# Weights and token chunks laid out as they lie on chip, and another order of the opening loads, splits and sums of squares

## The chip, the cores and the metric

One core of a Trainium2 chip runs the whole program. The metric is device time in microseconds (us) of that core; the kernel before takes 1963.29 us, the median of 3 runs (1960.71 to 1966.26). Engines are named as the profile names them: PE is TensorE, PEld its weight loads, DVE VectorE, ACT ScalarE, POOL GpSimd, SP the engine that issues every DMA of this kernel. A suffix q (SPq) marks an issue queue.

## The reference

One layer of a streaming encoder. `x_prompt` (2048 tokens of 1024), `x_sample` (32 tokens) and 16 meta tokens are normalised (RMSNorm with gain `norm_g`) and go through one input projection `w_in` of 1024 x 4104:

```
u = rmsnorm(h, g_norm) @ w_in     # columns q_A k_A v_A g_A | q_B k_B v_B g_B | 8 forget values
oa = stick-breaking attention of 8 heads (A); ob = forgetting (softmax with decay) attention of 8 heads (B)
h = h + concat(oa * silu(ga), ob * silu(gb)) @ w_out
```

The prompt attends to itself behind the meta tokens, the sample also to 2048 cached rows. The outputs are the normalised `h`, all new k and v rows, and the log forget values. Everything is float32.

## The kernel before

All 2096 tokens lie in one reversed list: prompt, sample, meta. Every projection is done with split operands: a float32 value is written as a high part (rounded to the format that TensorE multiplies at full rate) and a low part (the rest), and `mm3` (line 259) does three matmuls, high x high, high x low and low x high, for each of the 8 slices of 128 of the 1024 inputs. A group is therefore 24 matmuls into one PSUM bank.

The weights come in units of 256 columns (`load_unit`, line 178): two for each of q, k, v, g of both groups, and four of `w_out`. The first v unit of group B, v10, has 8 columns more, the forget values, which lie elsewhere in `w_in` and come in a second DMA. A unit is loaded in two halves (four slices of 128 rows each, so 1 KB pieces for each partition and slice), and each slice is split by ACT (line 205, the high part times the gain) and DVE (line 206, the low part). The half's raw buffer, `wraw`, exists once; for v10 the second half goes into `raw1`, one of two `raw` buffers that it shares with the token chunks.

The first section, v1, is the v projection of group B. The generator `feed` (line 1491) brings the tokens in 17 chunks of 128 (the last has 48). For chunk t it loads `x_T` into a `raw` buffer (4 KB for each partition), writes the high part (ACT, line 1504) and the low part (DVE, line 1505), squares both halves (ACT, line 1508), adds them up (three adds on POOL, lines 1509 to 1512), and some chunks later `root` sums over partitions with two small matmuls (`ptx`, line 1519) and finds the reciprocal root by a Newton step on DVE and ACT. The result of a group is copied out of PSUM with that root as scale (line 400), so a bank is free only when the chunk's root is there. PSUM has four banks for these groups.

The split chunks stay on chip ("resident") for v1, k1 and q1. `Pace` hands out the steps of `feed` against the steps of the projection: `advance(NL)` before the loop emits the first chunks, then every slice of matmuls advances it a little. Before all that, 40 matmuls on constant data (line 1549) run while the first loads come in. Later sections (k0, v0, q0, g0) fill the forgetting attention (`fx`), g1 and the output projections fill the stick-breaking attention; they read the tokens again through `stream` (line 606), in chunks of about 260 tokens from `x_K`, which is laid out as (128, 8, 2096), so a chunk comes in 1 KB pieces.

The order in which the code emits instructions is a priority. A scheduler then fixes the order on each engine from durations that it assumes, and may move an instruction ahead of earlier ones that wait; on chip each engine works strictly in that fixed order. Only in q1 are DVE and PE held to the order of the code.

Of the kernel before, what the change touches and what calls it, by code (L numbers as in the profile page):

```python
# [7 lines left out]
F32 = mybir.dt.float32  # L8
# [3 lines left out]
ALU = mybir.AluOpType  # L12
# [10 lines left out]
KT = 8  # L23
# [55 lines left out]
@with_exitstack  # L79
def trunk_step_kernel(ctx, tc, x_all, x_T, x_K, ca_kT, ca_v, cb_kT, cb_v, cb_lfT, norm_g, w_in, b_f, w_out,  # L80
                      final_g, ident_c, mask_c, smask_c, rows_c, pick_c,
# [7 lines left out]
    def dma(out, in_):  # L89
        nc.sync.dma_start(out=f32(out), in_=f32(in_))  # L90
# [86 lines left out]

    def load_unit(src, cols, kt, nm, g=None, raw1=None):

# [5 lines left out]
        def load(i):  # L185
            if i and raw1 is not None:
                raw[i] = raw1
# [93 lines left out]
    class SecT(Units):  # L281
        def __init__(self, nm, base, chunks, src, acc, evac, ahead=None, lead=0):
            super().__init__()
            self.nm, self.base, self.chunks, self.src, self.acc, self.evac = nm, base, chunks, src, acc, evac
            self.ahead, self.lead = ahead, lead
            self.every = 1 if lead else 2
            self.upto = 0
            self.next = None

        def unit(self, u):  # L290
            b = self.base + 256 * u
            return load_unit([w_in[:, b:b + 256]], 256, KT, f"{self.nm}{u}", g_col)

# [84 lines left out]
    class SecV(Units):  # L378
# [5 lines left out]
        def unit(self, u):  # L384
            s = self.s
            base = SECS * s + 2 * SEC
            cols = [w_in[:, base + 256 * u:base + 256 * u + 256]]
            if s and u == 0:
                cols.append(w_in[:, 2 * SECS:2 * SECS + 8])
            return load_unit(cols, 264 if s and u == 0 else 256, KT, f"v{s}{u}", g_col, self.raw1 if u == 0 else None)  # L390

# [214 lines left out]
    def stream(nm, a, n):  # L606
# [838 lines left out]

    k0 = SecT("k0", SEC, CH_K, stream, ps_a, evac_k(0))
    q0 = SecT("q0", 0, CH_Q, stream, ps_a, evac_q(0))
    v0 = SecV(0, CH_V, stream, ps_a)
    g0 = SecT("g0", 3 * SEC, CH_Q, stream, ps_a, evac_g(0))
    g1 = SecT("g1", SECS + 3 * SEC, CH_Q, stream, ps_a, evac_g(1), ahead_g)  # L1450

    class OutUnits(Units):
# [20 lines left out]
    with ExitStack() as es:  # L1473
# [17 lines left out]
        def feed():  # L1491

            todo = []
            for t in range(NT):
# [12 lines left out]
                for i in range(2):  # L1507
                    nc.scalar.activation(sq[i].rearrange("p (k c) -> p k c", k=4), raw[:, 4 * i:4 * i + 4], AF.Square)
                nc.gpsimd.tensor_tensor(sq[0], sq[0], sq[1], ALU.add)
                nc.gpsimd.tensor_tensor(sq[0][:, :2 * r], sq[0][:, :2 * r], sq[0][:, 2 * r:], ALU.add)  # L1510
                out = n_p.tile([128, 128], F32, tag="ss", name=f"ss{t}", bufs=3)[:, :r]
                nc.gpsimd.tensor_tensor(out, sq[0][:, :r], sq[0][:, r:2 * r], ALU.add)
# [4 lines left out]
                def root(t=t, r=r, ss=out):
                    pt = ps_t.tile([128, SEC], F32, tag="pt", name=f"ptx{t}")
                    nc.tensor.matmul(pt[:r, 0:1], ss, ones_t[:, 0:1], start=True, stop=True)
                    v = n_p.tile([128, 2], F32, tag="rs", name=f"rs{t}")  # L1520
                    newton(v[:r, 0:1], r_all[:r, t:t + 1], v[:r, 1:2], pt[:r, 0:1])
                    rooted.append(t)
                todo.append(root)
                yield 1.0 - HB
            for f in todo:
# [37 lines left out]
        ng.advance(NL)  # L1563
        for c in v1.run():
# [193 lines left out]
```

## Time and profile before

| | |
|---|---|
| median of 3 runs | 1963.29 us (1960.71 to 1966.26) |
| the profiled execution | 1965.0 us, of which the span of the trace is 1963.2 us |
| PE busy | 1885.2 us (96%) |
| DVE, POOL, ACT busy | 1294.2, 1166.6, 1082.2 us |
| granted TensorE clock, mean | 0.985 |
| DMA | 330.51 MB in 260107 packets, mean 168 GB/s |

Busy means that an instruction was running; for PE a busy share near 100% still allows for the lower clock. The granted clock is 1.00 at 2.4 GHz and 0.50 at 1.2 GHz. The idle time in square brackets of a timeline row is how long the engine had waited before that instruction, with what ended the wait.

### The profile page before, as it was taken

Reading aid. Unit: us, or ns where it says so; the run is one execution under the profiler, and the core shown is the slowest. Engines: PE = TensorE matmul, PEld = TensorE weight load, DVE = VectorE, ACT = ScalarE, POOL = GpSimd, SP = SyncE. Lnnn points to the kernel's source line nnn. Section 1 sums busy time; section 2 is a strip of 40 time slices with the busy share of each in tenths; the row PEclk is TensorE's granted clock in tenths of the full one; section 3 lists DMA queues with packets and bytes.
Section 4 is the critical chain, followed back from the end, with each engine's and each line's share of the span. In section 5 each row is a group of like instructions: output and inputs, shape, how many; then the busy total and the mean of one; then the engine's idle time right before and its main releaser. Section 6 shows DMA issues by size and latency. Waiting matters only on the chain.

```text
span 1963.2 us, 35618 instructions
## 1 busy us (share of the span) xinstructions
PE 1885.2 (96%) x11962; PEld 1479.7 (75%) x11962; DVE 1294.2 (66%) x2387; ACT 1082.2 (55%) x2327; POOL 1166.6 (59%) x1755
## 2 busy tenths in 40 slices
PE   8999999999999999999999999999999899999998
PEld 6999998677767777677777788777777666676566
DVE  5436336656674444766665376888878977878976
ACT  5541213454554554544453566776776777777852
POOL 4500003677777877676875676667777667667700
PEclk7999999999999999999999999999999999999999
DMA  6656657566664455566666544565656534434364
GB/s 164 183 134 151 172 155 192 139 186 164 187 165 132 134 171 169 173 200 198 216 201 195 173 152 156 173 213 181 200 167 204 174 123 151 152 109 154 98 206 165
DMA packets 260107, 330.51 MB, mean 168 GB/s; under 512 B 46525, under 2 KB 195094, under 8 KB 253782
## 3 DMA queue, kind: packets, MB, share of 16 engines
q1 hardware_dynamic: 259926, 328.25, 56.6%
q8 instruction: 94, 1.54, 0.3%
q14 instruction: 87, 0.71, 0.1%
HBM read 211.48 MB, written 116.68 MB: 167 GB/s over the span
## 4 chain that ended last, share of the span: by engine, by line
PE 58%; DVE 9%; DMA 5%; ACT 4%; POOL 3%; issue 3%; SPq 1%; DVEq 0%; ACTq 0%; POOLq 0%
PE pob L702 6%; PE poa L702 5%; PE pta L841 4%; PE sb L1151 3%; PE sb L1152 3%; PE smb L1128 3%; DVE wa L748 2%; PE sa L783 2%; PE sa L782 2%; PE psTg L262 2%; PE psTg L263 2%; PE psTg L264 2%; DMA gfa<-gf_s 2%; PE psTq L262 1%; PE psv L262 1%
## 5 line engine op out<-in xcount | busy, mean ns | idle before, releaser
L754 POOL TENSOR_TENSOR wa<-wa,mba 128x512 f32<-128x512 f32 (+1 forms) x320 | 369.4, 1156 | 172.5 <-DVE wa L748 145.3
L1165 POOL TENSOR_TENSOR accb<-accb,pfb 128x512 f32<-128x512 f32 (+1 forms) x256 | 297.4, 1162 | 103.2 <-ACT pfb L1155 75.4
L748 DVE TENSOR_TENSOR_SCAN wa<-sa,wa,ones_r 128x512 f32<-128x512 f32 x192 | 244.3, 1279 | 42.2 <-ACT sa L745 35.0
L1155 ACT ACTIVATE pfb<-sb 128x512 f32<-128x512 f32 (+1 forms) x320 | 176.0, 552 | 156.6 <-PE sb L1152 152.2
L1131 DVE TENSOR_REDUCE mxb<-smb 128x1 f32<-128x512 f32 (+1 forms) x320 | 194.7, 612 | 75.0 <-PE smb L1128 70.4
L844 ACT COPY ptha<-pta 128x512 f32<-128x512 f32 (+1 forms) x320 | 166.5, 526 | 81.1 <-PE pta L841 78.6
L744 ACT ACTIVATE mba<-sa 128x512 f32<-128x512 f32 (+1 forms) x320 | 174.0, 544 | 25.2 <-POOL wa L754 19.9
L841 PE MATMUL pta<-ident,wa 128*128 128x128 f32 x1088 | 173.4, 275 | 5.8 <-ACT ptha L844 3.2
L745 ACT ACTIVATE sa<-sa 128x512 f32<-128x512 f32 (+1 forms) x320 | 173.7, 543 | 0.0
L702 PE MATMUL poa<-ptha,vca 128*64 128x512 f32 (+2 forms) x640 | 157.7, 558 | 10.1 <-ACT ptha L844 9.8
L841 PEld LDWEIGHTS pta<-ident,wa 128*128 128x128 f32 x1088 | 129.7, 140 | 41.1 <-issue 8.2
L782 PE MATMUL sa<-kca,qaa 128*128 128x512 f32 (+3 forms) x352 | 150.3, 427 | 8.8 <-DVE wa L748 7.8
L262 PE MATMUL psTg<-xhg,whig 128*128 128x260 f32 x512 | 148.6, 290 | 0.0
L702 PE MATMUL pob<-pfb,vcb 128*64 128x512 f32 (+1 forms) x640 | 148.6, 569 | 0.0
L264 PE MATMUL psTg<-xhg,wlog 128*128 128x260 f32 x512 | 145.0, 283 | 0.0
L263 PE MATMUL psTg<-xlg,whig 128*128 128x260 f32 x512 | 144.8, 283 | 0.0
L1128 PE MATMUL smb<-k2b,q2b 66*128 66x512 f32 (+1 forms) x320 | 123.2, 385 | 14.3 <-DVE mxb L1131 9.3
L748 DVE TENSOR_TENSOR_SCAN wa<-sa,ones_r,m 128x512 f32<-128x512 f32 (+3 forms) x128 | 111.9, 878 | 36.5 <-ACT sa L745 23.8
L1151 PE MATMUL sb<-qab,kcb 128*128 128x512 f32 (+1 forms) x320 | 123.3, 385 | 0.7 <-ACT pfb L1155 0.7
L783 PE MATMUL sa<-kca,qz 128*128 128x512 f32 (+3 forms) x352 | 121.8, 358 | 0.0
L1152 PE MATMUL sb<-q2b,k2b 70*128 70x512 f32 (+1 forms) x320 | 121.4, 380 | 0.0
L702 PEld LDWEIGHTS poa<-ptha,vca 128*64 128x64 f32 x640 | 41.9, 137 | 86.1 <-issue 38.3
(296 smaller groups left out, 5408.9 us busy)
## 6 DMA issues: line engine op xcount, KB each, us to landing
xlg<-x_s SPq DMA_DIRECT2D x16, 1040.0 KB
xhg<-x_s SPq DMA_DIRECT2D x16, 1040.0 KB
xwk<-in_x_K_dram SPq DMA_DIRECT2D x8, 1048.0 KB
k_s<-kx SPq DMA_DIRECT2D x64, 131.0 KB
xwq<-in_x_K_dram SPq DMA_DIRECT2D x8, 1040.0 KB
x_s<-xhq SPq DMA_DIRECT2D x8, 1040.0 KB
x_s<-xlq SPq DMA_DIRECT2D x8, 1040.0 KB
q_s<-q SPq DMA_DIRECT2D x64, 130.0 KB
```

The lines of the kernel that those rows point to most:

```text
L262: nc.tensor.matmul(out, a_h[k], b_h[k], start=(k == 0), stop=False)
L263: nc.tensor.matmul(out, a_h[k], b_l[k], start=False, stop=False)
L264: nc.tensor.matmul(out, a_l[k], b_h[k], start=False, stop=(k == n - 1))
L702: nc.tensor.matmul(po[64 * side:64 * side + 64, :n], v, p[:, :n], start=first, stop=False)
L748: nc.vector.tensor_tensor_scan(out=w[:, 1:n + 1], data0=ps[:, :n], data1=m01[:, :n] if diag else ones_t[:, 0:1].broadcast_to([128, n]), in ...
L754: nc.gpsimd.tensor_tensor(w[:, :n], w[:, :n], take[:, :n], ALU.mult)
L782: nc.tensor.matmul(out, self.qa[:, bs], k, start=True, stop=False)
L841: nc.tensor.transpose(pt[:, b * 128:b * 128 + 128], self.w[b][:, c:c + 128], ident)
L1128: nc.tensor.matmul(ps[:, :SEC - s0 + m], q2[0:66, bs], k2[0:66, s0:SEC + m], start=True, stop=True)
L1131: nc.vector.tensor_reduce(mx[:, b, kc:kc + 1], ps[:, v0:v0 + nv + m], AX.X, ALU.max)
L1151: nc.tensor.matmul(ps[:, :n], hd.k[kc][:, js], self.qa[:, :n], start=True, stop=False)
L1165: nc.gpsimd.tensor_tensor(self.acc[:, :n], self.acc[:, :n], pf[:, :n], ALU.add)
```

## The change

The host writes two inputs in another order, with no arithmetic. `w_K` holds all 20 units one behind the other, for each partition first the four slices of half 0, then those of half 1; the 8 forget columns stand inside v10. `x_K`, `x_V` and `x_Q` hold the token chunks of `stream` in the same way, one copy for each of the three ways to cut them. A half of a unit is then one DMA of 128 pieces of 4 KB, a chunk one of 128 pieces of about 8 KB. The amount of data is the same.

```diff
-            r3 = raw[i][:, :kt // 2 * cols].rearrange("p (k c) -> p k c", k=kt // 2)
-            c = 0
-            for a in src:
-                w = a.shape[1]
-                dma(r3[:, :, c:c + w], a.rearrange("(i k p) c -> i p k c", p=128, i=2)[i])
-                c += w
+            n = kt // 2 * cols
+            dma(raw[i][:, :n], w_K[:, W_AT[nm] + i * n:W_AT[nm] + i * n + n])
...
-            dma(t["xw"][:, :KT * n].rearrange("p (k t) -> p k t", k=KT), x_K[:, :, a:a + n])
+            x = {"k": x_K, "v": x_V, "q": x_Q}[nm[0]]
+            dma(t["xw"][:, :KT * n], x[:, KT * a:KT * a + KT * n])
```

In `feed`, half of the chunks go into the `hl` staging buffers instead of `raw` (chunks 1, 2, 4, 5, 8, 9, ...), so four chunks can be under way. The squares of a chunk are emitted one chunk later, behind the splits of the next one.

```diff
-                raw = n_p.tile([128, 4 * 264], F32, tag="raw", name=f"xraw{t}")[:, :KT * r]
+                if t == 0 or t == 3 or t > 3 and (t - 4) // 2 % 2:
+                    raw = rawtile(f"xraw{t}")[:, :KT * r]
+                else:
+                    raw = f32(stage2(f"xraw{t}", SEC).rearrange("p x n -> p (x n)"))[:, :KT * r]
...
                 sub(xl, raw, xh)
-                sq = [stage(f"sq{t}_{i}", F32, "sg")[:, :4 * r] for i in range(2)]
...
+                if t == 0:
+                    yield 0.0
+                if last_:
+                    squares(*last_)
+                last_ = (t, r, raw)
                 yield HB
```

At the start there are 16 constant matmuls. Chunk 0 is split ahead of the weights. Both halves of v11, the second unit, are requested after chunk 1 (`NA`) instead of within the loop; both units use `raw` buffers for their second half. `NL`, the chunks emitted ahead of the loop, goes from 3.5 to 4.

```diff
-WARM = 40
+WARM = 16
-NL = 3.5
+NL = 4.0
+NA = 2.0
...
-        v1.raw1 = n_p.tile([128, 4 * 264], F32, tag="raw", name="raw1")
+        v1.raw1 = rawtile
         v1.prepare(0)
         dma(g_col, norm_g)
         v1.prep.pop(0)()
-        dma(ident, ident_c)
         v1.prep.pop(1)()
         next(ng)
-        nc.vector.tensor_copy(ident16, ident)
+        dma(ident, ident_c)
         v1.ready()
         v1.prepare(1)
         ng = Pace(ng)
-        ng.advance(NL)
+        ng.advance(NA)
+        nc.vector.tensor_copy(ident16, ident)
+        v1.prep.pop(0)()
+        v1.prep.pop(1)()
+        ng.advance(NL - NA)
```

## Rows read from the trace of the kernel before

**Rows 1.** The page, part 1: busy us (share of span) xinstructions.
```profile
PE 1885.2 (96%) x11962; PEld 1479.7 (75%) x11962; DVE 1294.2 (66%) x2387; ACT 1082.2 (55%) x2327; POOL 1166.6 (59%) x1755
```
**Rows 2.** Stretches of 10 us: length, engines' busy us (count), clock, DMA share, GB/s.
```profile
20.00:30.00 10.00, 7.31 (x33) 7.00 (x33) 8.01 (x14) 7.04 (x14) 6.85 (x6) 0.50 0.72 180
...
40.00:50.00 10.00, 9.51 (x56) 9.30 (x55) 5.28 (x16) 3.50 (x8) 2.15 (x4) 0.66 0.74 204
```
**Rows 3.** Tiles psv and ptx: count, ns min/median/max, first and last start us.
```profile
L262 PE MATMUL psv<-whiv,xh x272: 276/282/589, 12.7 to 131.7; 128*128 128x264 f32 x64, 128*128 128x256 f32 x64, 128*48 128x264 f32 x4, 128*48 128x256 f32 x4
...
L1519 PE MATMUL ptx<-ones_r,ss x34: 164/250/373, 12.6 to 106.4; 128*128 128x1 f32 x32, 128*48 128x1 f32 x2
```
**Rows 4.** Timeline, PE: first and last matmul of a group at full clock, twice.
```profile
115.10 0.28 PE L262 MATMUL psv<-whiv,xh 128*48 128x264 f32 x1
...
117.88 0.28 PE L264 MATMUL psv<-whiv,xl 128*48 128x264 f32 x1
118.00 0.28 PE L262 MATMUL psv<-whiv,xh 128*128 128x256 f32 x1
...
120.70 0.28 PE L264 MATMUL psv<-whiv,xl 128*128 128x256 f32 x1
```
**Rows 5.** Timeline of the opening: start, duration, engine, line, operation, count, idle before.
```profile
0.80 0.39 SPq L90 DMA_DIRECT2D xraw<-in_x_T_dram  x1
...
1.56 11.18 PE L1549 MATMUL warm<-masks 128*128 128x512 bf16 x40 [1.56 <-DVE masks L143]
...
3.99 2.61 SPq L90 DMA_DIRECT2D raw<-in_w_in_dram  x2
...
4.28 1.04 ACT L1504 CAST xh<-xraw 128x1024 fp32r<-128x1024 f32 x1 [1.98 <-DMA xraw<-in_x_T_dram]
...
5.36 1.22 DVE L93 TENSOR_TENSOR xl<-xraw,xh 128x1024 fp32r<-128x1024 f32 x1 [3.86 <-ACT xh L1504]
...
6.53 5.71 PEld L1549 LDWEIGHTS <-masks 128*128 128x128 bf16 x27 [0.16 <-issue]
...
11.62 1.74 ACT L205 ACTIVATE whiv<-wrawv,g_col 128x264 fp32r<-128x264 f32 x4 [5.24 <-DMA wrawv<-in_w_in_dram]
...
14.33 0.68 SPq L90 DMA_DIRECT2D rows<-in_rows_c_dram  x1
...
17.41 1.73 ACT L205 ACTIVATE whiv<-raw,g_col 128x264 fp32r<-128x264 f32 x4 [4.06 <-DMA raw<-in_w_in_dram]
...
19.70 2.04 SPq L90 DMA_DIRECT2D xraw<-in_x_T_dram  x2
```
**Rows 6.** Stretches of 1 us, columns as in rows 2.
```profile
3.00:4.00 1.00, 1.00 (x4) 0.30 (x2) 0.00 (x0) 0.00 (x0) 0.00 (x0) 1.00 0.98 326
...
9.00:10.00 1.00, 1.00 (x7) 0.41 (x6) 0.00 (x0) 0.00 (x0) 0.05 (x1) 1.00 0.82 103
...
27.00:28.00 1.00, 1.00 (x6) 1.00 (x6) 1.00 (x1) 0.62 (x1) 0.92 (x2) 0.50 0.92 87
```
**Rows 7.** Waits of PE, 0 to 170 us: total us, times, longest us.
```profile
PE psv L262 <- ACT whiv L205: 5.1, 2, 3.5
PE ptx L1519 <- POOL ss L1512: 2.9, 2, 2.7
```
**Rows 8.** Timeline, ACT ahead of the second unit's last split.
```profile
29.59 0.63 ACT L1508 ACTIVATE sq<-xraw 128x512 f32<-128x512 f32 x1 [1.57 <-POOL ss L1512]
...
38.95 0.49 ACT L205 ACTIVATE whiv<-wrawv,g_col 128x256 fp32r<-128x256 f32 x1
```
**Rows 9.** Timeline where q1 ends and k0 begins.
```profile
316.12 1.71 ACT L205 ACTIVATE whik<-wrawk,g_col 128x256 fp32r<-128x256 f32 x4 [5.25 <-DMA wrawk<-in_w_in_dram]
...
320.06 0.50 PE L1128 MATMUL smb<-k2b,q2b 66*128 66x512 f32 x1 [2.97 <-DVE mxb L1131]
```
**Rows 10.** Stretches of 5 us after it, columns as in rows 2.
```profile
320.00:325.00 5.00, 4.94 (x25) 4.89 (x26) 3.62 (x11) 0.42 (x1) 0.63 (x2) 0.66 0.94 237
...
350.00:355.00 5.00, 2.24 (x12) 1.84 (x13) 4.87 (x11) 0.00 (x0) 1.43 (x2) 0.96 0.19 40
```

More of the change, by code (lines that the diff above doesn't have):

```diff
@@ L62 @@
 MW = 2
-NL = 3.5
+NL = 4.0
+NA = 2.0
 LAG = 2
 NR = 5000.0
-WARM = 40
+WARM = 16
 CH_R = [(0, 384), (384, 384), (768, 384), (1152, 384), (1536, 560)]
 CH_V = [(c * 256, 256) for c in range(7)] + [(1792, 304)]
+COLS = {"q0": 0, "k0": SEC, "v0": 2 * SEC, "g0": 3 * SEC, "q1": SECS, "k1": SECS + SEC, "v1": SECS + 2 * SEC,
+        "g1": SECS + 3 * SEC}
+W_AT, W_ALL = {}, 0
+for _nm in [f"{x}{u}" for x in COLS for u in range(2)] + ["o00", "o01", "o10", "o11"]:
+    W_AT[_nm] = W_ALL
+    W_ALL += KT * (264 if _nm == "v10" else 256)
 def f32(ap):
@@ L186, in load @@
             if i and raw1 is not None:
-                raw[i] = raw1
+                raw[i] = raw1()
             else:
@@ L281, in trunk_step_kernel, with __init__ @@
     class SecT(Units):
-        def __init__(self, nm, base, chunks, src, acc, evac, ahead=None, lead=0):
+        def __init__(self, nm, chunks, src, acc, evac, ahead=None, lead=0):
             super().__init__()
-            self.nm, self.base, self.chunks, self.src, self.acc, self.evac = nm, base, chunks, src, acc, evac
+            self.nm, self.chunks, self.src, self.acc, self.evac = nm, chunks, src, acc, evac
             self.ahead, self.lead = ahead, lead
@@ L290, in unit @@
         def unit(self, u):
-            b = self.base + 256 * u
-            return load_unit([w_in[:, b:b + 256]], 256, KT, f"{self.nm}{u}", g_col)
+            return load_unit(256, KT, f"{self.nm}{u}", g_col)
         def first_x(self):
@@ L385, in unit @@
             s = self.s
[L386 to L390, printed above, removed]
+            return load_unit(264 if s and u == 0 else 256, KT, f"v{s}{u}", g_col, self.raw1)
         def first_x(self):
@@ L1444, in chunk @@
             todo.pop()()
[L1446 to L1447 removed]
+    k0 = SecT("k0", CH_K, stream, ps_a, evac_k(0))
+    q0 = SecT("q0", CH_Q, stream, ps_a, evac_q(0))
     v0 = SecV(0, CH_V, stream, ps_a)
[L1449 to L1450 removed]
+    g0 = SecT("g0", CH_Q, stream, ps_a, evac_g(0))
+    g1 = SecT("g1", CH_Q, stream, ps_a, evac_g(1), ahead_g)
     class OutUnits(Units):
@@ L1493, in feed, with squares, root @@
             todo = []
+            def squares(t, r, raw):
+                sq = [stage(f"sq{t}_{i}", F32, "sg")[:, :4 * r] for i in range(2)]
+                for i in range(2):
+                    nc.scalar.activation(sq[i].rearrange("p (k c) -> p k c", k=4), raw[:, 4 * i:4 * i + 4], AF.Square)
+                nc.gpsimd.tensor_tensor(sq[0], sq[0], sq[1], ALU.add)
+                nc.gpsimd.tensor_tensor(sq[0][:, :2 * r], sq[0][:, :2 * r], sq[0][:, 2 * r:], ALU.add)
+                ss = n_p.tile([128, 128], F32, tag="ss", name=f"ss{t}", bufs=3)[:, :r]
+                nc.gpsimd.tensor_tensor(ss, sq[0][:, :r], sq[0][:, r:2 * r], ALU.add)
+                def root():
+                    pt = ps_t.tile([128, SEC], F32, tag="pt", name=f"ptx{t}")
+                    nc.tensor.matmul(pt[:r, 0:1], ss, ones_t[:, 0:1], start=True, stop=True)
+                    v = n_p.tile([128, 2], F32, tag="rs", name=f"rs{t}")
+                    newton(v[:r, 0:1], r_all[:r, t:t + 1], v[:r, 1:2], pt[:r, 0:1])
+                    rooted.append(t)
+                todo.append(root)
+            last_ = None
             for t in range(NT):
                 r = rows_of(t)
-                raw = n_p.tile([128, 4 * 264], F32, tag="raw", name=f"xraw{t}")[:, :KT * r]
+                if t == 0 or t == 3 or t > 3 and (t - 4) // 2 % 2:
+                    raw = rawtile(f"xraw{t}")[:, :KT * r]
+                else:
+                    raw = f32(stage2(f"xraw{t}", SEC).rearrange("p x n -> p (x n)"))[:, :KT * r]
                 dma(raw, x_T[:, t * KT * 128:t * KT * 128 + KT * r])
@@ L1505, in feed @@
                 sub(xl, raw, xh)
-                sq = [stage(f"sq{t}_{i}", F32, "sg")[:, :4 * r] for i in range(2)]
[L1507 to L1512, printed above, removed]
+                if t == 0:
[3 more added lines that the diff above has]
+                last_ = (t, r, raw)
                 yield HB
@@ L1515, in feed @@
                     todo.pop(0)()
[L1517 to L1523, printed above, removed]
                 yield 1.0 - HB
+            squares(*last_)
             for f in todo:
@@ L1549, in trunk_step_kernel, with rawtile @@
             nc.tensor.matmul(warm, masks16[:, :128], masks16, start=(i == 0), stop=(i + 1 == WARM))
+        raws = []
+        def rawtile(nm="wraw1"):
+            raws.append(nm)
+            return n_p.tile([128, 4 * 264], F32, tag="raw", name=f"{nm}_{len(raws)}")
         ng = feed()
         next(ng)
-        v1.raw1 = n_p.tile([128, 4 * 264], F32, tag="raw", name="raw1")
+        v1.raw1 = rawtile
         v1.prepare(0)
@@ L1711 @@
     blocks = [x_all[t * 128:t * 128 + 128].reshape(-1, KT, 128).transpose(2, 1, 0).reshape(128, -1) for t in range(NT)]
+    w_in, w_out = a["w_in"][0], a["w_out"][0]
+    units = {f"{x}{u}": w_in[:, c + 256 * u:c + 256 * u + 256] for x, c in COLS.items() for u in range(2)}
+    units["v10"] = _np.concatenate([units["v10"], w_in[:, 2 * SECS:2 * SECS + 8]], axis=1)
+    units.update({f"o{s}{u}": w_out[SEC * s:SEC * s + SEC, SEC * u:SEC * u + SEC] for s in range(2) for u in range(2)})
+    units = _np.concatenate([units[n].reshape(-1, 128, units[n].shape[1]).transpose(1, 0, 2).reshape(128, -1)
+                             for n in W_AT], axis=1)
     ins = {
@@ L1714 @@
         "x_T": _np.concatenate(blocks, axis=1),
-        "x_K": x_all.reshape(T, KT, 128).transpose(2, 1, 0),
+        **{f"x_{x}": _np.concatenate([x_all[c:c + n].reshape(n, KT, 128).transpose(2, 1, 0).reshape(128, -1)
+                                      for c, n in ch], axis=1) for x, ch in (("K", CH_K), ("V", CH_V), ("Q", CH_Q))},
         "ca_kT": a["cache_a_k"][0, 0, ::-1].reshape(NX, SEC).T,
@@ L1721 @@
         "norm_g": a["norm_g"].reshape(KT, 128).T,
-        "w_in": a["w_in"][0],
+        "w_K": units,
         "b_f": a["b_f"],
-        "w_out": a["w_out"][0],
         "final_g": a["final_g"],
```

10 lines of the change are left out of this document (5 added, 5 removed).

## The prediction

> **What bounds the kernel now.** I read the busy shares first, then the clock and busy time by stretches, then the opening by timeline and DMA rate, then who PE waited for. PE is busy 96% of the span and the next engine 66% [rows 1]: the time is PE's work plus the places where PE stands still or runs at the lower clock. So the question for each edit is whether it closes such a place. The change touches two.
>
> The first is the opening. Section v1 runs from 12.7 to 131.7 us [rows 3], 119.2 us with the last matmul's end. Its work at full clock: 3 lines of 272 matmuls each are 816, half with 264 columns and half with 256. 23 intervals of the first kind take 117.88 - 115.10 = 2.78 us, 0.121 each; of the second 2.70 us, 0.1174 each [rows 4]. That is 408 x 0.121 + 408 x 0.1174 = 97.3 us, and the 34 `ptx` matmuls [rows 3] at the same spacing make 4.1 more: 101.4 us. So 17.8 us are lost inside v1, behind a start at 12.7. Where: PE waited 5.1 us for weight splits of ACT and 2.9 us for POOL's sums [rows 7]. The granted clock was 0.50 through 20 to 30 us, where 7.31 us of PE work cost 3.65 us more than at full clock, and 0.66 over 40 to 50, which is 6.8 us at half and 3.4 us lost [rows 2]. These are 15.1 us; the rest lies at 18 to 20 us, also at half, and in small waits.
>
> Behind both waits stand loads. The halves of v10 are requested at 1.7 and 3.99 us and split from 11.62 and 17.41 us, ACT having idled 5.24 and 4.06 us for them [rows 5]. While they move, the DMA engines are 0.82 busy at only 103 GB/s; the token chunk before them, in 4 KB pieces, moved at 326 GB/s at 0.98 [rows 6]. v11's second half arrives at 87 GB/s and 0.92 busy, without any 8-column pieces [rows 6], so the 1 KB pieces alone are slow. Chunks 2 and 3 cannot be requested before 19.70 us [rows 5], as both `raw` buffers are taken. The last split of v11 stands on ACT at 38.95 us, behind squares that wait 1.57 us for POOL [rows 8]; PE waits for it, and the clock falls again.
>
> The second place is the step from q1 to k0. The second half of k00 is requested at 310.44 us and split at 316.12, ACT having waited 5.25 us; q's cast stands behind it on ACT, the running maximum on DVE behind that, and PE stands 2.97 us [rows 9] and then runs for a while at 0.66 [rows 10].
>
> **The change part by part.**
>
> *Warming matmuls, 40 to 16.* The first 13 take 6.53 - 1.56 = 4.97 us, 0.38 each, the last 27 of them 5.71 / 27 = 0.21 [rows 5]. Sixteen take 13 x 0.38 + 3 x 0.21 = 5.6 us and end near 7.2 us. The clock has risen by then, as the spacing shows.
>
> *v10's loads.* Each half is 128 x 1056 x 4 = 541 KB. At 326 GB/s it takes 1.66 us. Chunk 0 was usable at 4.28 us [rows 5]; its request, g_col's and then v10's keep their order, so the halves are usable near 5.9 and 7.6 us, estimates from these rows. ACT splits four slices in 1.74 us: 5.9 to 7.7, then to 9.4. DVE follows one slice behind, as before, and is free from 5.36 + 1.22 = 6.6 us. PE needs 3 x 0.121 = 0.36 us for a slice, less than ACT's 0.43, so it starts at 7.3 us, follows the splits and ends group 0 near 10.2, 0.3 us later than its work alone. At the slow end the pieces gain only half: 0.2 MB per us instead of 0.326 puts the halves at 7 and 9.7 and the start at 7.5, with 2.5 us of waiting in the group.
>
> The Trainium skill's page "DMA: Bandwidth & Descriptors", section Specifications, puts the smallest transfer that runs at line rate at 512 bytes. By it the 1 KB pieces were at full rate already and the layout would bring nothing here; the row with 87 GB/s at 0.92 busy disagrees, and the measurement decides. What the time would be by that rule is the second rival.
>
> *Squares one chunk later, chunk 0 split first.* Between chunk 0 and the weights ACT no longer does two squares; the second group now needs chunk 1 only as high part (ACT, 1.04 us, 9.4 to 10.45) and low part (DVE, 1.22 us [rows 5], to 11.7). PE waits 1.4 us there. The squares themselves keep their number and lie beside PE's work; without that cover they show as `ptx` waits, 2.9 us before [rows 7].
>
> *Four chunk buffers.* Chunk 2 is requested right behind chunk 1, near 4 us instead of 19.70, so it is there by 12 us, when group 2 starts at 14.6. Nothing is added on an engine; the `hl` buffers are otherwise used in v1 only for the last chunk.
>
> *v11's two loads ahead of the loop.* They are two issues on SP at about 0.4 us. The first waits for the `wraw` buffer until DVE has split half 0 of v10 (8.3 us), the second for chunk 0's buffer until ACT has squared it (11.6 us). Behind them on SP stand the requests for chunks 2 and 3; if the order of the code holds there, chunk 2 comes near 15.5 us and group 2 waits up to 3 us. But the scheduler moves requests that do not wait ahead of those that do: `rows`, emitted with chunk 6, was issued at 14.33, ahead of chunk 2 [rows 5]. At 326 GB/s the halves are usable near 12 and 15.5 us. Their eight slices need 3.5 us of ACT and must be done for group 3 near 17.5 us. ACT's list from 9.4 us is three high parts (3.1), three pairs of squares (3.4) and these 3.5, 10 us, and the squares also wait for POOL [rows 8]. So the cost lies between 0 and today's 1.5 + 2.9 us; I take 1.5.
>
> *The clock.* With 1.4 and 1.5 us of waiting apart from each other there may be no fall at all (0); as much as today is 7 us. I take 2, nearer to none, since today's falls came with waits of 3.5 and of 1.5 plus more.
>
> Sum for v1: 7.3 + 101.4 + 0.3 + 1.4 + 1.5 + 2.0 = 113.9 us against 131.9, a gain of 18.0. Ends: 7.3 + 101.4 + 1.7 = 110.4 (gain 21.5) and 7.5 + 101.4 + 2.5 + 1.4 + 4.4 + 7 = 124.2 (gain 7.7).
>
> *k00's second half in 4 KB pieces.* Its 0.52 MB at 326 GB/s take 1.6 us, at 103 GB/s 5.1: 3.5 us less alone. Other transfers share the queue then, so I take 2.5 us, and 2.5 of the 2.97 us go, and with them perhaps the half clock (0.34 / 0.5 x 5 = 3.4 us at half, 1.7 us lost). What is late next is DVE's own row of splits. Between 0 and 4.7; I take 3.
>
> *All other units and chunks.* They are requested ahead, and PE is at 10.00 of 10 us around most of them; cover is the prefetch. Zero, between -5 and +5: the scheduler's order in the attention stages changes with the assumed durations of some 60 loads. How the stalls there look: 350 to 355 us, 2.24 us of PE work in 5 [rows 10], while DVE splits weights.
>
> Total: 18 + 3 + 0 = 21 us off the profiled execution's 1965.0 us: 1944. The median of the runs shown is 1.7 us lower than that execution, so the same gain from the median is 1942.3. I predict 1943.
>
> **The rivals.**
> 1. *Half the gain is given back in v1* (chance 0.22). ACT stands behind POOL's sums, v11's last slices come late again, PE waits about 4.4 us in all and the clock falls for about 14 us as today: v1 ends near 122, a gain of 10, with 1 at k0: 1954. For it: rows 8 show ACT held by POOL, and one chunk of delay does not make POOL faster. Against it: v11 is there some 15 us earlier and no longer emitted within the loop.
> 2. *The layout does not speed the loads* (0.05). Then the first weights come at 11.6 us, PE idles 4.3 us behind 16 warming matmuls and starts at half clock; the earlier chunks 2 and 3 save the 2.9 us of `ptx` waits at most: 1962. This is what the time would be if 1 KB pieces ran at full rate already. Against it: 87 against 326 GB/s.
> 3. *Slower: the scheduler's new order costs more in the attention stages than the opening gains* (0.04). Place: the ten units of k0 to g1, split by DVE while POOL and DVE also serve the attention. Price: one bad burst, as at 350 us, costs 2.76 us of idle in 5 and about as much on either side and in clock, some 6 us. From four more bad bursts out of ten on (24 us against 21) it decides; with four to five, 1965 - 21 + 27 = 1971. For it: the order is replanned. Against it: the steps and their counts there are the same, and the bursts of today stay as likely.
>
> **How the numbers follow.** The forecast, 1943, holds 0.69. Its own span is 1931 to 1951 (all best ends: 21.5 + 4.7 + 5 = 31; the loss side down to 14). The first rival reaches to 1957; I take 1931 to 1956 as the range for 8 in 10. About 0.3%, 5.9 us, is what a measurement of this kernel can tell from no change. Faster than 1957.4: the forecast and most of rival 1, 0.88. Within: rival 2 and the weak end of rival 1, 0.08. Slower: rival 3, 0.04.
>
> **What would show it.** The first `psv` matmul near 7.3 us and v1's last near 114; v10's halves split by ACT near 6 and 7.7; the DMA rate from 2 to 8 us near 326 GB/s; clock 1.00 in 20 to 30 us. At the end of q1 ACT's wait for `wrawk` near 2.5 us and PE's under 1. The prediction is wrong if the first projection matmul comes after 11 us (loads), if v1 ends after 122 us although it starts at 7 (splits, sums or clock), or if v1 ends at 114 and the total does not follow (later stages).

## The result and the profile after

The changed kernel takes 1949.12 us (median of 5, 1948.37 to 1955.18) against 1962.85 for the kernel before on the same chip (median of 5, 1960.71 to 1966.26): ratio 0.9936, interval 0.9919 to 0.9952, so 13.7 us faster. Run again (e0_after below) it takes 1948.81 against 1968.35, ratio 0.9905 (0.9892 to 0.9919). The profiled execution took 1949.0 us, its span is 1946.9, its mean clock 0.988.

The page's first part, as in [rows 1]: PE has 24 matmuls and 12.0 us less, its share is the same.

```profile
PE 1873.2 (96%) x11938; PEld 1473.1 (76%) x11938; DVE 1293.0 (66%) x2387; ACT 1081.9 (56%) x2327; POOL 1170.6 (60%) x1755
```

The opening's timeline, as in [rows 5] (start, duration, engine, line, operation, idle before):

```profile
1.55 6.05 PE L1562 MATMUL warm<-masks 128*128 128x512 bf16 x16 [1.55 <-DVE masks L151]
...
2.19 0.43 SPq L98 DMA_DIRECT2D wraw<-in_w_K_dram  x1
2.67 0.43 SPq L98 DMA_DIRECT2D ident<-in_ident_c_dram  x1
...
5.19 1.14 ACT L1498 ACTIVATE sq<-xraw 128x512 f32<-128x512 f32 x2
...
7.72 1.74 ACT L209 ACTIVATE whiv<-wrawv,g_col 128x264 fp32r<-128x264 f32 x4 [1.38 <-DMA wrawv<-in_w_K_dram]
...
8.29 0.39 PE L266 MATMUL psv<-whiv,xh 128*128 128x264 f32 x1 [0.69 <-ACT whiv L209]
...
9.36 1.72 ACT L209 ACTIVATE whiv<-wraw,g_col 128x264 fp32r<-128x264 f32 x4
```

The first half of v10 is split at 7.72 us instead of 11.62, the second at 9.36 instead of 17.41, with no wait between them. The stretch 2 to 10 us with its DMA rate, the one behind it, the two in which the clock was 0.50 and 0.66 before [rows 2], and the next:

```profile
2.00:10.00 8.00, 7.16 (x24) 3.08 (x23) 2.95 (x5) 4.66 (x11) 2.52 (x3) 1.00 0.93 327
10.00:20.00 10.00, 7.96 (x60) 7.21 (x60) 9.81 (x24) 9.93 (x20) 3.55 (x4) 1.00 0.68 230
20.00:30.00 10.00, 8.10 (x67) 7.74 (x66) 6.24 (x13) 4.99 (x11) 8.12 (x8) 1.00 0.55 187
...
40.00:50.00 10.00, 8.12 (x69) 7.92 (x67) 2.35 (x5) 4.25 (x8) 5.37 (x5) 1.00 0.85 267
50.00:60.00 10.00, 9.48 (x67) 9.48 (x68) 5.23 (x13) 6.47 (x14) 7.45 (x8) 0.83 0.52 163
```

The loads move at 327 GB/s and the clock is full up to 50 us. But PE stands for 1.9 us in each of the stretches from 20 and from 40 us, and from 10 to 20 us ACT and DVE are busy for 9.93 and 9.81 of 10. Section v1 (tile psv, as in [rows 3]) starts 4.4 us earlier and ends 9.2 us earlier; what PE waited for from 0 to 170 us, as in [rows 7] (total us, times, longest):

```profile
L266 PE MATMUL psv<-whiv,xh x272: 276/282/415, 8.3 to 122.5; 128*128 128x264 f32 x65, 128*128 128x256 f32 x63, 128*48 128x264 f32 x4, 128*48 128x256 f32 x4
```
```profile
PE ptx L1506 <- POOL ss L1502: 5.6, 3, 2.4
PE psv L266 <- ACT vt L399: 2.2, 2, 1.4
...
PE psv L268 <- DVE xl L101: 0.7, 2, 0.5
PE psv L266 <- ACT whiv L209: 0.7, 1, 0.7
```

The 5.1 us for weight splits have become 0.7, which stand ahead of v1's first matmul, but the 2.9 us for POOL's sums have become 5.6, and 2.2 for evacuations (`vt`, the copy that needs the root) are new. The second place, from q1 to k0, answers to [rows 9]:

```profile
304.06 1.71 ACT L209 ACTIVATE whik<-wrawk,g_col 128x256 fp32r<-128x256 f32 x4 [3.30 <-DMA wrawk<-in_w_K_dram]
...
308.00 0.50 PE L1128 MATMUL smb<-k2b,q2b 66*128 66x512 f32 x1 [0.87 <-DVE mxb L1131]
```

PE's 2.97 us are 0.87, and no half clock follows (1.00 from 310 to 315 us, where [rows 10] has 0.66). The gains add up along the span: 9.2 us at the start of k1, 13.6 at q1's end, 14.0 at k0's, 16.5 at q0's, 22.0 at g1's, 19.2 at the end of the first output projection, 16.3 at the end of the span. These are differences of two profiled executions, one of each kernel.

### The profile page after: what moved, and what is told of

Same layout as the page of the kernel before. It is cut to its first block, busy times and chain, and to the rows that moved or that the text cites. A ratio compares the mean times of both kernels' runs of the same rounds, so it can differ in the third digit from the quotient of the medians.

```text
span 1946.9 us, 35559 instructions
## 1 busy us (share of the span) xinstructions
PE 1873.2 (96%) x11938; PEld 1473.1 (76%) x11938; DVE 1293.0 (66%) x2387; ACT 1081.9 (56%) x2327; POOL 1170.6 (60%) x1755
## 4 chain that ended last, share of the span: by engine, by line
PE 61%; DVE 9%; DMA 5%; ACT 3%; POOL 3%; issue 3%; SPq 1%; DVEq 0%; ACTq 0%; POOLq 0%
PE pob L702 6%; PE poa L702 5%; PE pta L841 5%; PE sb L1151 3%; PE smb L1128 3%; PE sb L1152 3%; DVE wa L748 2%; PE sa L783 2%; PE sa L782 2%; PE psTg L266 2%; PE psTg L268 2%; PE psTg L267 2%; PE psTq L266 2%; PE psv L266 1%; PE psTq L268 1%
## 5 line engine op out<-in xcount | busy, mean ns | idle before, releaser
L1128 PE MATMUL smb<-k2b,q2b 66*128 66x512 f32 (+1 forms) x320 | 123.0, 385 | 9.6 <-DVE mxb L1131 4.9
```

What stands on the lines that cost most here:

```text
L1128: nc.tensor.matmul(ps[:, :SEC - s0 + m], q2[0:66, bs], k2[0:66, s0:SEC + m], start=True, stop=True)
```

## The experiments

The table has every run beside the kernel before and after: when v1's first matmul and k1's first matmul start, what v1 lost (its length less the 101.4 us of work of the prediction), and the time. The rows from e1 to e4 shared one chip, as did e0, e6, e8 and e9, then e12 and e14, then e15 and e9b; each ratio is to the kernel before on that chip.

| kernel | v1 from | k1 from | lost in v1 | median us | ratio (95%) |
|---|---|---|---|---|---|
| before | 12.7 | 132.0 | 17.9 | 1962.85 | |
| after | 8.3 | 122.8 | 13.1 | 1949.12 | 0.9936 (0.9919 to 0.9952) |
| e0_after | 7.7 | 122.8 | 13.7 | 1948.81 | 0.9905 (0.9892 to 0.9919) |
| e1_layout_only | 12.0 | 123.4 | 10.0 | 1949.16 | 0.9913 (0.9883 to 0.9943) |
| e2_order_only | 13.0 | 131.5 | 17.1 | 1967.64 | 1.0017 (0.9998 to 1.0035) |
| e3_const_late | 8.1 | 119.6 | 10.1 | 1946.68 | 0.9901 (0.9871 to 0.9931) |
| e4_warm40 | 12.4 | 122.6 | 8.8 | 1944.75 | 0.9896 (0.9862 to 0.9931) |
| e6_w_layout | 8.3 | 123.4 | 13.7 | 1951.86 | 0.9925 (0.9909 to 0.9941) |
| e8_sums_cut | 7.0 | 112.2 | 3.8 | 1937.86 | 0.9847 (0.9827 to 0.9867) |
| e9_late_warm40 | 12.5 | 118.9 | 5.0 | 1944.37 | 0.9881 (0.9866 to 0.9896) |
| e9b_late_warm40 | 13.1 | 119.3 | 4.8 | 1942.80 | 0.9878 (0.9860 to 0.9896) |
| e12_dve_add | 13.1 | 115.9 | 1.4 | 1940.62 | 0.9871 (0.9851 to 0.9890) |
| e14_layout_late | 13.2 | 123.2 | 8.6 | 1947.36 | 0.9914 (0.9889 to 0.9938) |
| e15_dve_add_warm16 | 8.2 | 115.2 | 5.6 | 1943.20 | 0.9874 (0.9853 to 0.9895) |

**Which part of the change pays: e1_layout_only and e2_order_only.** The first is the kernel before with the new inputs alone, the second the changed kernel with the old ones.

```diff
 # e1: before, with w_K, x_K, x_V, x_Q and their loads; order, NL = 3.5, WARM = 40 as before
 # e2: after, but
-            dma(raw[i][:, :n], w_K[:, W_AT[nm] + i * n:W_AT[nm] + i * n + n])
+            for a in wsrc(nm): ... dma(r3[:, :, c:c + w], a.rearrange("(i k p) c -> i p k c", p=128, i=2)[i])
-            dma(t["xw"][:, :KT * n], x[:, KT * a:KT * a + KT * n])
+            dma(t["xw"][:, :KT * n].rearrange("p (k t) -> p k t", k=KT), x_K[:, :, a:a + n])
```

> The kernel before with the two layouts alone (weights by unit, token chunks of the later sections by chunk); order of loads, splits and squares, two chunk buffers and 40 warming matmuls as before. Theory L (the loads make the gain): the splits of v10 come near 8 and 9.5 us instead of 11.6 and 17.4, but the 40 matmuls hold PE until 12.2, so the first projection matmul stays near 12.4 and the wait of 3.5 us for the second half goes; v1 ends near 125 (7 us earlier), PE's wait at the end of q1 falls from 2.97 to about 0.9 us, total 1951 to 1955. Theory O (the new order makes the gain): v1 ends within 2 us of 131.9 and the total stays at 1960 to 1964.

> The changed kernel with both layouts as before (1 KB pieces, the 8 forget columns in a DMA of their own); order, four chunk buffers and 16 warming matmuls as changed. Theory L: the first split of v10 is again near 11.5 and the second near 17 us, PE stands 4 us behind the 16 warming matmuls and again for the second half, the clock falls to 0.50; v1 ends within 3 us of 131.9, PE's wait at the end of q1 is back near 3 us, total 1958 to 1965. Theory O: v1 ends near 124 and the total is within 4 us of the changed kernel's 1949.

Measured: the layout alone gives what the whole change gives (1949.16, a little below the 1951 to 1955 expected; k1 from 123.4), the order alone gives nothing (1967.64, somewhat above the 1958 to 1965 expected, ratio 1.0017; k1 from 131.5). With the old inputs the first weights come at 12.48 us and PE, whose 16 warming matmuls are done, stands 6.45 us and then runs at 0.56; the timeline and the stretch of e2 show it:

```profile
12.48 1.73 ACT L221 ACTIVATE whiv<-wrawv,g_col 128x264 fp32r<-128x264 f32 x4 [5.85 <-DMA wrawv<-in_w_in_dram]
...
13.05 0.59 PE L278 MATMUL psv<-whiv,xh 128*128 128x264 f32 x1 [6.45 <-ACT whiv L221]
```
```profile
8.00:9.00 1.00, 0.00 (x0) 0.00 (x0) 0.00 (x0) 0.00 (x0) 0.88 (x2) 1.00 0.67 84
...
10.00:20.00 10.00, 5.99 (x24) 5.42 (x24) 4.18 (x12) 4.76 (x10) 0.00 (x0) 0.56 0.80 174
```

In e1 the order of the opening is the old one and one large wait is left: the last split of v11 stands on ACT behind two squares that wait 1.04 and 1.56 us for POOL, as in [rows 8]. The second of these squares and the split on ACT, and PE's wait:

```profile
30.88 0.63 ACT L1508 ACTIVATE sq<-xraw 128x512 f32<-128x512 f32 x1 [1.56 <-POOL ss L1512]
31.42 0.49 ACT L209 ACTIVATE whiv<-wrawv,g_col 128x256 fp32r<-128x256 f32 x1
```
```profile
31.96 0.39 PE L266 MATMUL psv<-whiv,xh 128*128 128x256 f32 x1 [3.91 <-ACT whiv L209]
```

The new order takes this wait away and puts others in its place: inside v1 PE waits 8.7 us in all in the changed kernel and 6.4 in e1. In both, POOL's sums have a part in the largest waits.

**What holds ACT at 37 us: e3_const_late. What an earlier start of PE is worth: e4_warm40.** In the changed kernel ACT stands 5.34 us and POOL 7.82, in the middle of v1:

```profile
35.68 3.98 SPq L98 DMA_DIRECT2D kb_s<-one  x5
...
42.76 0.64 ACT L1498 ACTIVATE sq<-xraw 128x512 f32<-128x512 f32 x1 [5.34 <-DMA kb_s<-one]
...
43.48 1.29 POOL L1499 TENSOR_TENSOR sq<-sq,sq 128x512 f32<-128x512 f32 x1 [7.82 <-ACT sq L1498]
...
50.52 0.38 PE L1506 MATMUL ptx<-ones_r,ss 128*128 128x1 f32 x2 [2.39 <-POOL ss L1502]
```

`constants()` fills a tile `one` and stores it five times; the tile comes from the two staging buffers of the squares, so the next square waits until the stores have read it. The roots that follow are late, and PE waits 2.39 us at 50.52. e3 emits the constants behind the last chunk, e4 puts the 40 warming matmuls back.

```diff
 # e3
-                if t == 6:
-                    constants()
...
             dma(r_s, row)
+            constants()
 # e4
-WARM = 16
+WARM = 40
```

> The changed kernel with one call moved: the constants (masks, ones rows) are emitted behind the last chunk's root instead of with chunk 6. Theory S (the constants hold the squares' two staging buffers until the DMA of the ones rows has read them, 5.34 us on ACT at 37 to 43 us, and the sums stay behind from there): the wait of 5.3 us on ACT goes, PE's waits of 2.39 us at 50.5, 1.44 at 65.4 and 0.77 at 78 us go with the half clock at 51 to 55 us; v1 ends near 116 instead of 122.8, total 1941 to 1944. Rival P (POOL's rate of sums is the bound, 2.5 to 4.3 us for a chunk, wherever the constants stand): the waits come at other chunks with the same sum, v1 ends at 121 to 123, total within 2 us of 1949.

> The changed kernel with 40 warming matmuls instead of 16. The theory of the prediction (with the weights there, the warming matmuls beyond those that bridge the loads stand on PE's path): PE is held until 12.2 instead of 7.6 us, the first projection matmul comes at 12.3 instead of 8.3; ACT and DVE go on splitting meanwhile, so the first groups wait less and about 2.5 of the 4 us stay: v1 ends near 125, total 1951 to 1953. Rival (the opening is set by ACT's and POOL's chain, not by PE's start): v1 ends within 1 us of 122.8 and the total is within 2 us of 1949.

With the constants late k1 starts 3.2 us earlier than after, half of what theory S expected, and PE's waits for sums fall from 5.6 to 3.2 us. e3 gives the 3.2 us back by the end of k0 (its last matmul starts at 550.1, after at 550.0). e4 is the telling one: PE starts 4.1 us later than after, and k1 starts at the same time, 122.6. An earlier first matmul is worth nothing here, since the end of v1 hangs on other engines. The totals of e3 and e4 lie 2 to 4 us below e0, but on another chip; against the kernel before on the same chip their ratios, 0.9901 and 0.9896, are not told apart from e0's 0.9905.

**Is it POOL's sums: e8_sums_cut, with e0_after beside it.**

```diff
 # e8: e3, and
-                    nc.scalar.activation(sq[i]..., raw[:, 4 * i:4 * i + 4], AF.Square)
+                    nc.scalar.activation(sq[i]..., raw[:, 4 * i:4 * i + 4], AF.Square, scale=2.0)
-                nc.gpsimd.tensor_tensor(sq[0], sq[0], sq[1], ALU.add)
-                nc.gpsimd.tensor_tensor(sq[0][:, :2 * r], sq[0][:, :2 * r], sq[0][:, 2 * r:], ALU.add)
-                nc.gpsimd.tensor_tensor(ss, sq[0][:, :r], sq[0][:, r:2 * r], ALU.add)
+                nc.gpsimd.tensor_tensor(ss, sq[0][:, :r], sq[1][:, r:2 * r], ALU.add)
```

> The changed kernel itself once more, beside the three that follow on one chip. Expected of every theory: 1948 to 1951 us, v1 to 122.5, k1 from 122.8. If it comes at 1945 or below, the earlier distance of 2 to 4 us to the variants with the constants late and with 40 warming matmuls was the chip and not the kernel.

> The changed kernel with the constants emitted behind r_s (as e3_const_late), and with one add of one eighth on POOL for each chunk's squares instead of three adds: six of the eight squares are left out of the sum, and the two that remain are scaled by four. PE's matmuls, ACT's squares and the loads keep their number. Theory 1 (v1 is set by the chain squares on ACT, sums on POOL, roots, evacuations): with POOL's work cut from about 2.5 us to 0.4 a chunk, PE's waits for sums (5.6 us in the changed kernel) go to under 1 us, with them the fall of the clock, and k1 starts at 113 to 116 us instead of 119.6. Rival (ACT's own amount of work, high parts, squares, splits and evacuations, sets it, POOL only happens to be last): PE's waits move to ACT's evacuations and splits, and k1 starts at 118 to 120. In both the end of the kernel follows by less, since the k0 stage gave the last 3 us back in e3_const_late: 1941 to 1947.

PE's waits for sums go from 3.2 us (e3) to none, the fall of the clock goes, and k1 starts at 112.2 instead of 119.6, earlier even than expected. The whole list of PE's waits from 0 to 130 us in e8:

```profile
PE warm L1559 <- DVE masks L151: 1.6, 1, 1.6
PE psv L266 <- ACT xh L1522: 1.2, 1, 1.2
PE psv L268 <- DVE xl L101: 0.7, 1, 0.7
```

v1 starts 1.1 us earlier in e8 than in e3 and is some 6 us shorter. So without the three adds the waits are gone, though ACT has as many squares, splits and copies as in e3: ACT's amount of work alone does not hold v1. It does not follow that ACT has no part. The adds end a chain that begins with ACT's squares, and in the changed kernel POOL idles 4.06 and 3.14 us for squares of the opening; whether earlier squares would do as much as fewer adds was not tried. The time, 1937.86, is 11 us below e0 on the same chip. In the profiled executions e8 is 10.6 us ahead at k1 and 7.1 at the end.

**The two steps together: e9_late_warm40 and e9b_late_warm40.** The edits of e3 and e4 in one kernel; e9b is the same once more on another chip.

> The changed kernel with the constants emitted behind r_s and 40 warming matmuls, the two steps that each came out 2 to 4 us below the changed kernel. Theory 1 (v1's end is set by the sums' chain, not by PE's start): although PE starts at 12.4 instead of 8.1, k1 starts at 118 to 121 as with the constants late alone, and the time is 1942 to 1946. Rival (40 matmuls were harmless only because the constants held ACT up anyway): with the constants out of the way PE's later start shows, k1 starts near 123 and the time is 1946 to 1950.

> The kernel of e9_late_warm40 once more, beside the one with the first add on DVE. Expected of every theory: 1942 to 1946, k1 from 118.5 to 119.3.

k1 starts at 118.9 and 119.3, no later than with the constants late and 16 warming matmuls (119.6), though PE starts 4.4 us later. The rival, k1 near 123, is out. On e0's chip e9 takes 1944.37, 4.4 us less than the changed kernel, with each of its four times (1941.27 to 1946.05) below each of e0's (1948.50 to 1949.37).

**Weights or chunks: e6_w_layout.** The changed kernel with the old `x_K` for the later sections' chunks (the second edit of e2 alone).

> The changed kernel with the later sections' token chunks loaded as before (pieces of about 1 KB of the transposed input) and only the weights as they lie on chip. The opening, which uses neither, stays: k1 from 122.8, and q1's end gains its 4 us as in the changed kernel. The sections k0 to q0 and g0, g1 load 40 such chunks in the background. Theory 1 (loads there are hidden, PE is at 10 of 10 around them): 1948 to 1951, no change. Rival (the 3 to 5 us that the changed kernel gains in the projection of g0 and g1 come from the chunks' faster loads or fewer packets): those go back, 1952 to 1955.

1951.86 (1950.65 to 1956.12), 3 us above e0 on the same chip: the intervals of the two ratios overlap, but each of its five times is above each of e0's four. Along the span the difference is 0.6 us at k1's start, 2.2 at v0's end, 4.0 at q0's, 2.6 at g1's and 2.9 at the end. The sections g0 and g1 take 506 us in e6 and 508 in e0 (from the last matmul's start of q0 to that of g1), so their gain over the 511 of before does not come from the chunks. The chunks' layout is worth 3 us at most; the other 16 us below the kernel before come with the weights' layout, as the order alone gives nothing.

**Less on POOL without leaving work out: e12_dve_add and e15_dve_add_warm16. What the order is worth then: e14_layout_late.**

```diff
 # e12: e9 (constants late, WARM = 40), and
-                nc.gpsimd.tensor_tensor(sq[0], sq[0], sq[1], ALU.add)
+                (nc.vector if t > 1 else nc.gpsimd).tensor_tensor(sq[0], sq[0], sq[1], ALU.add)
 # e15: the same with WARM = 16
 # e14: e1 with the constants late as in e3
```

> The changed kernel with the constants behind r_s and 40 warming matmuls (e9_late_warm40), and from the third chunk on the first of the three adds of the squares on DVE instead of POOL; nothing is left out. POOL's chain for a chunk falls from 1.3 + 0.8 + 0.5 to 1.3 us, DVE gets about 0.7 us more a chunk, where it is busy some 6 of 10 us. Theory 1 (the chain of sums sets v1's end, as the cut sums showed): what PE still waits in v1 with e9_late_warm40, 1.9 for sums and 2.2 for evacuations, goes in part; k1 starts at 116 to 118 instead of 118.9, and the time is 1 to 3 us below that kernel's: 1940 to 1944. Rival (DVE is the next engine to be late in 10 to 30 us, with the splits and low parts): PE waits for DVE's low parts instead, k1 from 119 to 122, 1944 to 1948.

> Only the layout (the order of the opening, the squares and the 40 warming matmuls as before the change) and the constants behind r_s. Theory 1 (with the constants out of the way, PE's wait of 3.9 us for v11's splits behind ACT's squares remains, and only the new order takes it away): k1 starts at 121.5 to 123.5, 1946 to 1949, some 3 us above e9_late_warm40, and that is what the order is worth. Rival (the order is worth nothing even then): k1 starts at 119 or before and the time is 1943 to 1945.

> As e12_dve_add (constants behind r_s, first add of the squares on DVE from the third chunk on), but with the 16 warming matmuls of the changed kernel. Theory 1 (PE's earlier start is worth something only once the sums no longer set v1's end; with one wait of 1.4 us left in v1 they hardly do): PE starts near 8 us instead of 13.1 and k1 starts at 112.5 to 115 instead of 115.9, 1937 to 1941. Rival (the sums of chunks 0 and 1, still on POOL with all three adds, and PE's fixed place for their roots hold the opening): PE waits some 3 us for them again at 16 and 24 us, k1 starts at 115.5 to 118, and the time is that of 40 matmuls or above, 1940 to 1944.

e12 starts k1 at 115.9, a little earlier than expected, and of its 102.8 us in v1 all but 1.4 are work; these 1.4 us are its one wait, the sum of the third chunk. Its first add, now on DVE, stands behind two low parts, so that POOL idles 5.21 us for it, and POOL's next add takes 1.64 us instead of 0.74:

```profile
21.02 1.64 POOL L1500 TENSOR_TENSOR sq<-sq 128x256 f32<-128x256 f32 x1 [5.21 <-DVE sq L1499]
...
23.31 0.38 PE L1506 MATMUL ptx<-ones_r,ss 128*128 128x1 f32 x2 [1.39 <-POOL ss L1502]
```

It has the lowest time of the versions that leave nothing out, 1940.62 us, ratio 0.9871 (0.9851 to 0.9890). Its 3 us over e9 at k1 are read from the traces; in whole times the two aren't told apart (0.9881 and 0.9878, intervals that overlap). e15 starts PE 4.9 us earlier than e12 and k1 by 0.7: the waits return, 2.5 us for two sums and 1.2 for splits and low parts inside v1, behind 1.6 ahead of it, and the time is no better. e14 shows that the order does do something once the constants are out of the way: its k1 starts at 123.2, as expected, against 118.9 and 119.3 in e9 and e9b, since the wait for the last split remains:

```profile
31.97 0.58 PE L266 MATMUL psv<-whiv,xh 128*128 128x256 f32 x1 [3.91 <-ACT whiv L209]
```

In whole times e14 and e9 are not told apart (0.9914 and 0.9881, intervals that overlap). In the changed kernel itself the constants cancel what the order gives.

## Why the prediction was right and wrong

The time came out 6 us above the forecast and inside the range; the mechanism of v1 is that of the first rival (half given back, ACT behind POOL's sums, v1's end near 122), not that of the forecast. The prediction's own sign says the same: v1 starts at 8.3 us and ends at 123.0, after 122. That the time is nevertheless nearer to the forecast than to the rival's 1954 is in part luck: v1 gained half of what was forecast, k0 somewhat more, and 2.7 us came from later stages, for which no run shows a cause. And the forecast's own span is narrower than its terms: their low ends, 7.7 + 0 - 5, make a gain of 2.7 us, not 14. By the steps:

*The loads: the rate right, the times 1.8 us late.* Forecast 326 GB/s, measured 327. (The row at 326 GB/s in [rows 6] held 66 pieces of 1 KB beside 62 of 4 KB, so it was not the chunk alone.) The halves were split from 7.72 and 9.36 us, forecast 5.9 and 7.6: SP issued both, `ident` and chunk 1 within 1.4 us, so they shared the rate, and the first half did not have it alone. ACT squared chunk 0 ahead of the weights after all (5.19 us), since the scheduler moved the squares into the wait; that cost nothing, ACT still waited 1.38 us. Start 8.3 instead of 7.3, 7.0 to 8.3 in the runs with 16 warming matmuls and the new layout.

*The work: right.* 101.4 us stand: e12 needs 102.8, with 1.4 of wait. (Before, v1 with its last matmul's end is 119.4 us long, not 119.2.)

*The squares: the step that failed.* "The squares themselves keep their number and lie beside PE's work; without that cover they show as `ptx` waits": I saw the condition and priced it at nothing. The cover was gone. POOL's timeline in the changed kernel (start, duration):

```profile
13.15 1.28 POOL L1499 TENSOR_TENSOR sq<-sq,sq 128x512 f32<-128x512 f32 x1 [4.06 <-ACT sq L1498]
...
18.98 2.89 POOL L1499 TENSOR_TENSOR sq<-sq,sq 128x512 f32<-128x512 f32 x1 [3.14 <-ACT sq L1498]
21.94 0.73 POOL L1500 TENSOR_TENSOR sq<-sq 128x256 f32<-128x256 f32 x1
22.75 1.32 POOL L1502 TENSOR_TENSOR ss<-sq 128x128 f32<-128x128 f32 x1
24.81 1.31 POOL L1499 TENSOR_TENSOR sq<-sq,sq 128x512 f32<-128x512 f32 x1 [0.74 <-ACT sq L1498]
...
28.28 1.30 POOL L1499 TENSOR_TENSOR sq<-sq,sq 128x512 f32<-128x512 f32 x1 [0.74 <-ACT sq L1498]
```
```profile
15.89 0.38 PE L1506 MATMUL ptx<-ones_r,ss 128*128 128x1 f32 x2 [1.30 <-POOL ss L1502]
...
24.12 0.38 PE L1506 MATMUL ptx<-ones_r,ss 128*128 128x1 f32 x2 [1.90 <-POOL ss L1502]
```

Each chunk takes 2.5 us of adds or more, and then mostly 0.74 us until ACT has written the next square into the buffer that POOL just released: POOL and ACT take turns over two buffers. The first `ptx` that waits has its sum at 15.83 and the next at 24.07 us, and PE works in a fixed order in which each root has its place among the matmuls; the sum comes after that place. Once PE had the weights early, this chain became the late one. In the opening it is late for two reasons: POOL gets chunk 1's squares only at 13.15 us, as ACT has splits and high parts to do first, and chunk 2's three adds take 5.1 us, from 18.98 to 24.07, instead of 2.5 (the last section shows beside what). With its two waits, 1.30 and 1.90, the 2.39 behind the constants, the evacuations' 1.44 and 0.77, and 0.9 of small ones, PE stands 8.7 us; the clock, 0.83 from 50 to 60 us, is 3.4 us at half and 1.7 lost. The remaining 2.7 of the 13.1 lost are steps that ran slower, 0.9 in group 0, which follows the splits, and most of the rest in the three groups behind it (estimates from the timeline).

*The constants: not in the sum.* The change does not touch them, so I did not look at whose buffers they use. In the old order they move k1 by next to nothing (e1 against e14: 123.4 and 123.2, though v1 itself is 1.4 us shorter in e14, which starts later); in the new one they cost 3.2 us (after against e3).

*v11, its order on SP, the chunk buffers, the clock.* Chunk 2 was forecast to be requested near 4 us. Its request (the first of the three in the second row) stands behind that of v11's first half, which waits until DVE has split v10's first half:

```profile
10.22 0.33 SPq L98 DMA_DIRECT2D wrawv<-in_w_K_dram  x1
10.60 3.08 SPq L98 DMA_DIRECT2D xraw<-in_x_T_dram  x3
```

This cost PE 0.27 us, where up to 3 was named for that order. v11's splits cost no wait (1.5 forecast), chunk 1's low part 0.48 (1.4), the clock 1.7 (2.0). All of this is small beside the step above.

*The sum of v1:* gain 9.2 us instead of 18.0, within my ends of 7.7 and 21.5. e8 shows how much the two left-out terms were: with the sums cut and the constants late the gain is 19.8.

*k00's second half:* forecast 3, measured 4.4 between the start of k1 and q1's last matmul (196.6 us before, 192.2 after): 2.1 of PE's wait and 1.7 of the clock, which I had named without counting both in full. ACT's wait is 3.30 where I said near 2.5. The layout does it: 192.5 us in e1, 195.5 in e2, and 191.3 to 193.8 in all kernels with the weights' new layout.

*All other units:* forecast 0 with 5 on either side. Over the rest of the span the profile gains 2.7 us: about 3 from q1's end up to q0's and 5.5 in g0 and g1, less 5.7 behind that. In all kernels of the table, g0 and g1 take 505.5 to 511.8 us, and the same program differs by 2 (505.6 in after, 507.6 in e0), so these stages carry no sign of the change. The stall at 350 us [rows 10] is still there, now from 330 to 340 us, with PE busy for half of it:

```profile
330.00:335.00 5.00, 4.06 (x20) 2.10 (x20) 5.00 (x4) 2.10 (x6) 4.92 (x5) 1.00 0.02 7
335.00:340.00 5.00, 1.01 (x4) 0.71 (x5) 4.96 (x8) 0.00 (x0) 2.97 (x3) 0.76 0.00 0
```

The prediction laid it to DVE's splits. The rows show why they are long there, beside adds of the attention on POOL: seven splits take 9.47 us, while the median split of k0's weights takes 0.48.

```profile
328.95 9.47 DVE L210 SCALAR_TENSOR_TENSOR wlok<-wrawk,g_col,whik 128x256 fp32r<-128x256 f32 x7
...
332.47 5.66 POOL L1165 TENSOR_TENSOR accb<-accb,pfb 128x512 f32<-128x512 f32 x4
```

One loss at the end can be seen. In the last projection PE waits 2.83 us, with the clock at 0.91 from 1880 to 1900, since DVE waits for `yl` to be read back:

```profile
1886.42 0.69 DVE L1409 TENSOR_TENSOR yl<-psl,yl 128x512 f32<-128x512 f32 x1 [3.01 <-DMA yl<-y_s]
```
```profile
1887.17 0.77 PE L266 MATMUL psl<-whio,mxh 128*128 128x512 f32 x1 [2.83 <-DVE yl L1409]
```

Before, PE's wait there was 1.02 us. It is 2.16 in e0, 1.19 in e9, 1.11 in e1; why the read-back comes later in some kernels was not tried.

*The total:* 9.2 + 4.4 + 2.7 is the 16.3 us of the span; 16.0 between the profiled executions, against 21 forecast, and 13.7 between the medians, as the profiled execution of before lay 2.2 us above the median. The rival that the layout does not speed the loads is refuted by e1 and e2. Its price was fair: e2, with the slow loads and the new order, was put at 1962 and came out at no change. The slower rival did not happen: no variant came out slower than the kernel before by more than its interval.

## What to carry to other kernels

When a stage loses time to two chains that run side by side, pricing the repair of one needs the finish time of the other, worked out from its own rows (here at least 2.5 us of adds and 0.7 of hand-over a chunk, against PE's 2.8 us a group, of which the first three each take a new chunk; later a chunk serves two groups, and the sums catch up), not its wait in the old profile: that wait is small only because the first chain was later. An earlier start of the bounding engine was worth nothing here until the last producer of its inputs was earlier too; putting the warming matmuls back tests this in one run. And before an order is changed, list who else takes buffers from the pools that it uses: the constants, untouched by the change, took a third of what was missing.

## What the runs showed of the hardware

The same add of two 128 x 512 tiles on POOL took 1.26 to 1.31 us in most chunks, but 2.89 us from 18.98, while DVE ran two low parts; in turn a small DVE operation took 1.06 us beside it instead of 0.16. The timeline of DVE at that time:

```profile
18.36 2.36 DVE L101 TENSOR_TENSOR xl<-xraw,xh 128x1024 fp32r<-128x1024 f32 x2
20.63 0.16 DVE L569 RECIPROCAL r_all<-r_all 128x1 f32<-128x1 f32 x1
20.82 1.06 DVE L570 TENSOR_TENSOR rs<-r_all 128x1 f32<-128x1 f32 x1
```

POOL's add ends at 21.87, 1.15 us behind the end of the low parts, and DVE's small operation of two inputs ends with it, at 21.88, while the reciprocal, of one input, took its usual 0.16 beside the add: those of two inputs went nearly one behind the other. The Trainium skill's page "SBUF — State Buffer", section "SBUF: two separate sides", says that a DVE operation with two SBUF inputs and a GpSimd operation that reads SBUF share a pair of ports as an exclusive lock that the later one waits for in full; the rows agree. The splits of k0 beside POOL's adds, 1.35 us each instead of 0.48, are the same picture. That work should therefore not be moved from one to the other doesn't follow here: on DVE the add takes 0.68 us (median of 15 in e12), and e12 gained 3 us at k1 by moving it.

Loads in pieces of 4 KB moved at 327 GB/s; the first weights in pieces of 1 KB (with the 8-column pieces of v10 among them) at 84 GB/s with the DMA engines 0.67 busy (e2, 8 to 9 us). That is not a fixed rate of the 1 KB piece. In the same run, from 18 to 20 us, the same kind of pieces of v11 moved at 223 GB/s:

```profile
18.00:20.00 2.00, 2.00 (x10) 1.93 (x9) 1.76 (x7) 2.00 (x4) 0.00 (x0) 0.50 0.85 223
```

So the prediction's "1 KB pieces alone are slow" is too general. The new layout makes the pieces longer and also changes how far apart they lie in memory; no run separates the two, and what made the first loads slow stays open.
